# A hybrid Fourier and Hyena encoder layer on one core: real group's inverse transforms once each in fp32, sums by VectorE, and the filters' norms in the gates' convolution taps

## The chip, the cores and the metric

The kernel runs on one core of a Trainium2 chip. A core has five engines that matter here, each with its own queue that it works off in order: TensorE (PE; its weight loads are listed as PEld), VectorE (DVE), ScalarE (ACT), GpSimd (POOL) and SyncE (SP, which here only issues DMA). They share an on-chip memory, SBUF, of 128 partitions; TensorE writes its results to PSUM, from where VectorE and ScalarE read them. The metric is the device time of one execution in microseconds (us), as the median of several runs.

## The reference

The layer is applied to two sequences (x_prompt and x_sample) of 1024 positions and 1024 channels, with the same weights. The Hyena branch is where the change lies:

```python
    h = h * jnp.exp(-t[:, None, None, None] * jnp.abs(decay.astype(f32))[None])
    h = h / jnp.sum(jnp.abs(h), axis=(0, 1), keepdims=True)
    ...
    hv = short_conv(hv, w_short)
    v, x1, x2 = jnp.split(hv, 3, axis=-1)
    kf = hyena_filters(L, ...)
    z = v.astype(jnp.float32)
    for n, gate in enumerate((x1, x2)):
        z = gate.astype(jnp.float32) * long_conv(z, kf[:, n], hyena_d[n].astype(jnp.float32))
    y_h = (z.astype(dt) * jax.nn.silu(hg)) @ w_hyena_out
```

Each filter is divided by its norm, the sum of its absolute values over all positions and both directions, one number per order n and channel. `short_conv` is a depthwise convolution of width 3 over the sequence, `long_conv` a convolution of full length through a Fourier transform of 2048 points plus a skip term. Since the norm is one number per channel, and the short convolution is linear in its taps, the division can be done anywhere on the way to the product with the gate. Around this branch stand a Fourier branch, sigmoid merge gates, an output projection and norms; they are not touched.

## The kernel before

The work stands in stages: the Fourier branch and the norm of the input, then the filters with some of the gates' projections between them (up to some 700 us), then the convolutions (`branches`, about 705 to 1690 us), the remaining gate projections (`phase_gates`) and the output (`phase_out`).

Matrices that need more than one fp32r matmul gives are split: `split` makes a rounded high part h (a ScalarE cast) and a remainder l (a subtraction on VectorE, some on GpSimd), and `mm3` multiplies as h·H + h·L + l·H, three matmuls. Input projections (`inproj`, output tile pin) are 48 such matmuls of 512 columns for a tile of 128 channels.

`branches` runs through 32 steps: two batches, eight channel tiles c, two orders n. A step's long convolution has a front and a back. `conv_front` folds the sequence into even and odd parts, transposes them on TensorE (tph) and makes from them, in `butterfly`, the inputs of four frequency groups: group 0 is real, with one tile of fp32 numbers; groups 2, 1 and 3 are complex and split into bh and bl. `conv_back` (line 796) takes the groups in the order 0, 2, 1, 3. For each, `forward` multiplies with a cosine and sine table into PSUM (pX). Group 0 does that in true fp32 with four matmuls of 128 columns against the table cfw0 (line 596), the others with twelve fp32r matmuls of 256 columns. VectorE multiplies pX with the filter's spectrum (t, line 806) and adds (Y, line 810). Y is split into yh and yl (line 813), and twelve fp32r matmuls of 256 columns transform it back into PSUM (pT, line 833). For group 0 the table holds the cosine part of pair 0 used for both halves by broadcast, and that of pair 4 with both signs, so that PSUM ends with sum and difference next to each other. ScalarE copies the result to T0s (line 839); VectorE later forms U and V from T0s and group 2's result, and S and D from T1s and group 3's, then four sums q and the unfolded output y (yc).

A gate x1 or x2 is a projection, after which `conv` (line 754) applies the three taps of `wsh`: one ScalarE activation with the middle tap, two VectorE instructions for the outer ones. `gate` (line 862) multiplies the convolution's output with the gate and with `invn`, the reciprocal of the filter's norm, in one scalar_tensor_tensor on VectorE. `invn` is a tile of 16 columns, one per order and channel tile, filled by `filter_taps` (line 656), whose last column is written before the convolutions begin.

PSUM tiles named pT and tph come from one pool (tag "T") of two buffers, which are taken in turn: the two transposes of a front, then groups 0, 2, 1, 3 of a back. So group 1's transform writes to the bank that group 0's result was in. Tiles pX have two buffers of their own, pin two.

The order on each engine is not the order of this text. A scheduler places the instructions by an own estimate of their durations when the kernel is built, so a change of a few instructions can move others around it. SP issues the loads of filter spectra (k) and of weights, POOL computes the remainders of the projections' weights and stores and loads some of them.

Of the kernel before, what the change touches and what calls it, by code (L numbers as in the profile page):

```python
# [16 lines left out]
P = 128  # L17
# [29 lines left out]
def _tables():  # L47
    t = {}
    s = np.arange(P) + 0.5
    fwd, inv = [], []  # L50
    th = np.zeros((P, 8, 6))
    for pi, (f1, hf) in enumerate(PAIRS):
# [9 lines left out]
        if f1 == 0:  # L62
            inv += [ci, -si]
        elif f1 == 4:
            inv += [ci, -ci, -si, si]
        else:
            inv += [-si, ci, si]
# [10 lines left out]
    t["c_fwd"] = _hl(np.concatenate(fwd[4:], axis=1))  # L78
    t["c_inv"] = _hl(np.concatenate(inv, axis=1))
# [63 lines left out]
for _pi, (_f1, _hf) in enumerate(PAIRS):  # L143
    IOFF[_pi] = _o
    _o += 256 if _f1 == 0 else (512 if _f1 == 4 else 384)
# [16 lines left out]
class K:  # L162
# [633 lines left out]
    def conv_back(self, n, ct, B, ws):  # L796
# [3 lines left out]
        for g, pairs in GROUPS:  # L800
# [8 lines left out]
            Y = ws.tile([P, 2, 2, P], F32, tag="y", name="y", bufs=1)  # L809
            self.add("dve", Y, t[:, 0], t[:, 1, :, ::-1])  # L810
            yh = ws.tile([P, 2, 2, P], F32R, tag="yh", name="yh", bufs=2)
# [4 lines left out]
            for r in range(2):  # L816
                for i, pr in enumerate(pairs):
                    w = (yh[:, i, r], yl[:, i, r])
                    o = IOFF[pr]
                    if g == 0:  # L820
                        out = T4[:, r::2]
                        if i == 0:
                            R = [ci[:, hl, o + r * P:o + r * P + P].unsqueeze(1).to_broadcast([P, 2, P]) for hl in range(2)]
                        else:
                            R = [ci[:, hl, o + r * 256:o + r * 256 + 256].rearrange("p (a b) -> p a b", a=2)
                                 for hl in range(2)]
                    elif r == 0:
                        out = T4[:, 0::3]
                        R = [ci[:, hl, o + P:o + 3 * P].rearrange("p (a b) -> p a b", a=2) for hl in range(2)]
                    else:  # L830
                        out = T4[:, 1:3]
                        R = [ci[:, hl, o:o + 2 * P].rearrange("p (a b) -> p a b", a=2) for hl in range(2)]
# [4 lines left out]
            if g in (0, 1):  # L837
                T[g] = tt(f"T{g}s")
# [23 lines left out]
    def gate(self, n, ct, y, g):  # L862

        c = n * 8 + ct
        self.stt("dve", g, y, self.invn[:, c:c + 1], g, MUL, MUL)
        return g

    def phase_main(self, nct=8, nb=NB, nf=16):
        tc, nc, a = self.tc, self.nc, self.a
        with ExitStack() as es:  # L870
# [24 lines left out]
            for i in range(nf):  # L895
# [7 lines left out]
                if i == 2:  # L903
                    self.cinv = mi.tile([P, 2, INVW], F32R, name="cinv")
                if i in (2, 4, 6):
# [5 lines left out]
    def branches(self, nb, nct, ws):  # L911
# [3 lines left out]
        tc, nc = self.tc, self.nc  # L915
        steps = []
# [552 lines left out]
```

## Time and profile before

| what | value |
|---|---|
| median of 3 runs | 2442.94 us (2442.49 to 2445.35) |
| the profiled execution's own time | 2444.67 us |
| its span, first to last instruction | 2442.9 us |
| mean granted TensorE clock | 0.996 |
| TensorE busy | 2396.8 us (98%), 13196 matmul records |
| VectorE busy | 1896.5 us (78%) |
| ScalarE busy | 1096.7 us (45%) |
| GpSimd busy | 487.0 us (20%) |
| convolutions' transforms back (pT) | 1024 records with yh, 512 with yl |

The span is 2442.9 us, and the execution as a whole took 1.8 us more. Busy time counts the time in which an engine has at least one instruction under way; matmuls overlap, so the number of a group's records times their mean length is more than the group's time, and what a matmul costs is the distance from its start to the next one's. An fp32 matmul leaves two records, an fp32r matmul one. In rows of the timeline stand start, length, engine, source line, operation, tiles out<-in, shape and count; in rows by stage the stage's bounds and length, and for each engine busy time and count, then the granted clock, the share of the DMA engines and GB/s; in rows of waits, who waited for whom, the sum in us, how often, and the longest.

### The profile page before, as it was taken

The numbers are of one execution on the slowest core, as the hardware profiler recorded it, in microseconds if no ns is written. First come the engines' busy times: TensorE is split into PE (matmuls) and PEld (weight loads), VectorE is DVE, ScalarE is ACT, GpSimd is POOL, SyncE is SP. The second block draws the span as 40 slices with busy tenths as digits, with TensorE's granted clock in tenths as the row PEclk, the third lists the DMA queues.
The fourth block names the chain that finished last, engine by engine and source line by source line (L and its number), as shares of the span: only waits on it lengthen the run. The fifth ranks groups of instructions, "written<-read, shape, count | busy, mean of one in ns | idle before, by whom it ended". The sixth has DMA issues, their size and how long they took to land.

```text
span 2442.9 us, 36854 instructions
## 1 busy us (share of the span) xinstructions
PE 2396.8 (98%) x13196; PEld 2084.8 (85%) x13196; DVE 1896.5 (78%) x3405; ACT 1096.7 (45%) x2063; POOL 487.0 (20%) x518
## 2 busy tenths in 40 slices
PE   6999999999999999999999999999999999999998
PEld 5988888888888888888888888888788888888886
DVE  7687888888748999999989999766555455665677
ACT  5546577767633433334223323333344444544343
POOL 1341322222143433331000000112200012122111
PEclk9999999999999999999999999999999999999999
DMA  7535655555555555545444444335454567776543
GB/s 265 187 133 198 218 180 169 169 176 166 172 194 178 172 177 173 163 165 195 147 129 133 141 141 139 121 121 184 141 177 167 190 211 254 253 255 217 170 162 130
DMA packets 225823, 429.36 MB, mean 176 GB/s; under 512 B 23574, under 2 KB 87287, under 8 KB 225256
## 3 DMA queue, kind: packets, MB, share of 16 engines
q1 hardware_dynamic: 198444, 333.34, 42.5%
q0 software_dynamic: 27008, 93.65, 11.1%
q8 instruction: 104, 1.70, 0.3%
q14 instruction: 79, 0.65, 0.1%
q10 hardware_dynamic: 188, 0.02, 0.0%
HBM read 290.60 MB, written 136.31 MB: 175 GB/s over the span
## 4 chain that ended last, share of the span: by engine, by line
PE 92%; DMA 2%; DVE 2%; ACT 1%; issue 1%; POOL 1%; SPq 0%; DVEq 0%; ACTq 0%; POOLq 0%
PE pin L194 41%; PE pT L194 7%; PE pg L194 7%; PE pyf L194 7%; PE pyh L194 7%; PE pX L194 7%; PE po L194 6%; PE pXf L194 3%; PE pfv L194 2%; PE pft L194 1%; PE tph L792 1%; PE tpx L194 1%; DMA x<-in_x 1%; DMA wr<-in_w_fo 0%; DMA d_x<-xg 0%
## 5 line engine op out<-in xcount | busy, mean ns | idle before, releaser
L194 PE MATMUL pin<-xh,wl 128*128 128x512 f32 x1472 | 577.7, 392 | 3.3 <-POOL wl L181 3.3
L194 PE MATMUL pin<-xh,wh 128*128 128x512 f32 x1472 | 577.2, 392 | 0.9 <-DMA wh<-d_w 0.9
L194 PE MATMUL pin<-xl,wh 128*128 128x512 f32 x1472 | 576.2, 392 | 0.4 <-DVE xl L181 0.4
L181 POOL TENSOR_TENSOR wl<-wr,wh 128x512 fp32r<-128x512 f32 x136 | 240.8, 1772 | 1141.9 <-ACT wh L171 1108.1
L171 ACT CAST wh<-wr 128x512 fp32r<-128x512 f32 x264 | 163.5, 620 | 365.0 <-PE pin L194 141.3
L194 PEld LDWEIGHTS pin<-xh,wl 128*128 128x128 f32 x1472 | 277.5, 189 | 55.8 <-POOL wl L181 4.8
L194 PEld LDWEIGHTS pin<-xh,wh 128*128 128x128 f32 x1472 | 277.4, 188 | 52.5 <-DMA wh<-d_w 1.3
L194 PEld LDWEIGHTS pin<-xl,wh 128*128 128x128 f32 x1472 | 277.5, 189 | 52.2 <-DVE xl L181 1.0
L194 PE MATMUL pT<-cinv,yh 128*128 128x256 f32 x1024 | 193.1, 283 | 0.0
L194 PEld LDWEIGHTS pT<-cinv,yh 128*128 128x128 f32 x1024 | 164.0, 190 | 9.0
L181 DVE TENSOR_TENSOR t<-pX,k 128x1024 f32<-128x1024 f32 x128 | 155.7, 1216 | 11.0 <-PE pX L194 9.3
L181 DVE TENSOR_TENSOR wl<-wr,wh 128x512 fp32r<-128x512 f32 x128 | 87.8, 687 | 94.1 <-ACT wh L171 93.8
L194 PE MATMUL pX<-bh,cfwd 128*128 128x256 f32 x768 | 159.6, 286 | 0.0
L194 PE MATMUL pyf<-sf,wh 128*128 128x512 f32 x512 | 157.7, 389 | 0.0
L194 PE MATMUL pyh<-sh,wh 128*128 128x512 f32 x512 | 157.3, 389 | 0.0
L171 ACT CAST bh<-b 128x512 fp32r<-128x512 f32 x144 | 89.0, 620 | 126.0 <-DVE b L181 84.2
L194 PE MATMUL pT<-cinv,yl 128*128 128x256 f32 x512 | 144.9, 283 | 0.0
L171 ACT CAST yh<-y 128x512 fp32r<-128x512 f32 x128 | 79.2, 618 | 112.3 <-DVE y L181 89.5
L194 PEld LDWEIGHTS pX<-bh,cfwd 128*128 128x128 f32 x768 | 126.4, 190 | 2.5
L194 PEld LDWEIGHTS pyh<-sh,wh 128*128 128x128 f32 x512 | 96.1, 188 | 19.9
L194 PEld LDWEIGHTS pyf<-sf,wh 128*128 128x128 f32 x512 | 96.1, 188 | 19.9
L194 PE MATMUL pX<-bl,cfwd 128*128 128x256 f32 x384 | 109.6, 285 | 0.0
(354 smaller groups left out, 5262.9 us busy)
## 6 DMA issues: line engine op xcount, KB each, us to landing
k<-d_k SPq DMA_DIRECT2D x128, 512.0 KB, 4.0
wr<-in_w_in SPq DMA_DIRECT2D x136, 256.0 KB, 3.1
d_g<-gt SPq DMA_DIRECT2D x124, 256.0 KB, 2.8
d_k<-kt SPq DMA_DIRECT2D x128, 128.0 KB, 2.1
d_k<-kt SPq DMA_DIRECT2D x64, 256.0 KB, 2.3
wr<-in_w_fo POOLq DMA_DIRECT2D x64, 256.0 KB, 4.1
g<-d_g SPq DMA_DIRECT2D x64, 256.0 KB, 4.4
wr<-in_w_ho POOLq DMA_DIRECT2D x64, 256.0 KB, 4.0
```

The source lines that it names most:

```text
L171: self.rounded = nc.scalar.copy(h, src)
L181: return e.tensor_tensor(out, a, b, op=op)
L194: return self.nc.tensor.matmul(out, lhsT, rhs, start=start, stop=stop, skip_group_check=shared)
L792: nc.tensor.transpose(tp[:, q * P:(q + 1) * P], eo[:, e, q], self.ident)
```

## The change

Group 0's inverse tables leave `c_inv` and stand in a table of their own, `c_in0`, in plain fp32, with each of the four pieces once. In `conv_back`, group 0 no longer splits Y. Four fp32 matmuls of 128 columns put the two cosine products pair 0's two products (cosine and sine) side by side into the lower half of a PSUM tile (pT0) and pair 4's into its upper half; ScalarE copies the upper half of 256 columns to T0s, and VectorE adds it to the lower half and subtracts it from it, which gives the two halves of T0s, in the order that they had before. Y of group 0 (y0) lies in a buffer of the yl ring instead of y's only buffer. The tables for `c_inv` shrink from 3072 to 2304 columns in each part, loaded in three DMAs as before; `c_in0` is one more DMA on SP's queue, of 128 x 512 fp32 numbers.

The norms are multiplied once, ahead of the convolutions, into the taps of the sections of x1 and x2 (16 blocks of three columns of `wsh`), and `gate` becomes a plain product on VectorE.

```diff
--- before.py
+++ after.py
@@ -47,7 +47,7 @@
 def _tables():
     t = {}
     s = np.arange(P) + 0.5
-    fwd, inv = [], []
+    fwd, in0, inv = [], [], []
     th = np.zeros((P, 8, 6))
     for pi, (f1, hf) in enumerate(PAIRS):
         f = f1 + 8 * (np.arange(P) + P * hf)
@@ -59,10 +59,8 @@
             wt[0] = 1 / 2048.0
         fwd += [c, sn]
         ci, si = (c * wt).T, (sn * wt).T
-        if f1 == 0:
-            inv += [ci, -si]
-        elif f1 == 4:
-            inv += [ci, -ci, -si, si]
+        if f1 in (0, 4):
+            in0 += [ci, -si]
         else:
             inv += [-si, ci, si]
         ang = w * 127.5
@@ -76,6 +74,7 @@
             th[:, pi] = np.stack([ct, -st, 0 * ct, 0 * ct, st, 0 * ct], axis=1)
     t["c_fw0"] = np.concatenate(fwd[:4], axis=1).astype(np.float32)
     t["c_fwd"] = _hl(np.concatenate(fwd[4:], axis=1))
+    t["c_in0"] = np.concatenate(in0, axis=1).astype(np.float32)
     t["c_inv"] = _hl(np.concatenate(inv, axis=1))
     t["c_th"] = th.astype(np.float32)
 
@@ -142,7 +141,7 @@
 _o = 0
 for _pi, (_f1, _hf) in enumerate(PAIRS):
     IOFF[_pi] = _o
-    _o += 256 if _f1 == 0 else (512 if _f1 == 4 else 384)
+    _o += 0 if _f1 in (0, 4) else 384
 INVW = _o
 GROUPS = [(0, (0, 1)), (2, (4, 5)), (1, (2, 3)), (3, (6, 7))]
 KOFF = {0: 0, 1: 8, 2: 16, 3: 24}
@@ -806,8 +805,21 @@
             self.mul("dve", t.rearrange("p k h r c -> p k (h r c)"),
                      X.rearrange("p h r c -> p (h r c)").unsqueeze(1).to_broadcast([P, 2, 512]),
                      kt.rearrange("p (k a) b -> p k (a b)", k=2))
-            Y = ws.tile([P, 2, 2, P], F32, tag="y", name="y", bufs=1)
+            Y = ws.tile([P, 2, 2, P], F32, tag="y" if g else "yl", name="y" if g else "y0", bufs=1 if g else 2)
             self.add("dve", Y, t[:, 0], t[:, 1, :, ::-1])
+            if g == 0:
+
+                Tp = self.psum("T", 2, "pT0")
+                for i in range(2):
+                    for r in range(2):
+                        s = slice((2 * i + r) * P, (2 * i + r + 1) * P)
+                        self.mm(Tp[:, s], Y[:, i, r], self.cin0[:, s], True, True)
+                T[0] = ws.tile([P, 512], F32, tag="tt", name="T0s", bufs=4)
+                lo, hi = T[0][:, 0:256], T[0][:, 256:512]
+                nc.scalar.copy(hi, Tp[:, 256:512])
+                self.add("dve", lo, Tp[:, 0:256], hi)
+                self.sub("dve", hi, Tp[:, 0:256], hi)
+                continue
             yh = ws.tile([P, 2, 2, P], F32R, tag="yh", name="yh", bufs=2)
             yl = ws.tile([P, 2, 2, P], F32R, tag="yl", name="yl", bufs=2)
             self.split(yh, yl, Y, "dve", "act")
@@ -817,14 +829,7 @@
                 for i, pr in enumerate(pairs):
                     w = (yh[:, i, r], yl[:, i, r])
                     o = IOFF[pr]
-                    if g == 0:
-                        out = T4[:, r::2]
-                        if i == 0:
-                            R = [ci[:, hl, o + r * P:o + r * P + P].unsqueeze(1).to_broadcast([P, 2, P]) for hl in range(2)]
-                        else:
-                            R = [ci[:, hl, o + r * 256:o + r * 256 + 256].rearrange("p (a b) -> p a b", a=2)
-                                 for hl in range(2)]
-                    elif r == 0:
+                    if r == 0:
                         out = T4[:, 0::3]
                         R = [ci[:, hl, o + P:o + 3 * P].rearrange("p (a b) -> p a b", a=2) for hl in range(2)]
                     else:
@@ -834,8 +839,8 @@
 
             def tt(name):
                 return ws.tile([P, 512], F32, tag="tt", name=name, bufs=4)
-            if g in (0, 1):
-                T[g] = tt(f"T{g}s")
+            if g == 1:
+                T[g] = tt("T1s")
                 nc.scalar.copy(T[g], Tp)
             elif g == 3:
                 S_, D_ = tt("S"), T[1]
@@ -861,8 +866,7 @@
 
     def gate(self, n, ct, y, g):
 
-        c = n * 8 + ct
-        self.stt("dve", g, y, self.invn[:, c:c + 1], g, MUL, MUL)
+        self.mul("dve", g, y, g)
         return g
 
     def phase_main(self, nct=8, nb=NB, nf=16):
@@ -902,6 +906,8 @@
                     self.spill_gate(0, sec, c, ws)
                 if i == 2:
                     self.cinv = mi.tile([P, 2, INVW], F32R, name="cinv")
+                    self.cin0 = mi.tile([P, 4 * P], F32, name="cin0")
+                    nc.sync.dma_start(self.cin0, a["c_in0"])
                 if i in (2, 4, 6):
 
                     s = slice((2, 4, 6).index(i) * INVW // 3, ((2, 4, 6).index(i) + 1) * INVW // 3)
@@ -913,6 +919,8 @@
 
 
         tc, nc = self.tc, self.nc
+        gt = self.wsh.rearrange("p (m j) -> p m j", j=3)[:, 8:24]
+        self.mul("dve", gt, gt, self.invn.unsqueeze(2).to_broadcast([P, 16, 3]))
         steps = []
         for b in range(nb):
             steps.append((b, 0, 0))
```

The scheduler's order is another one from the first convolution on. Up to there TensorE's rows are the same, and after the convolutions too. The first place is TensorE at the ninth convolution of the first batch, at group 0's transform back. Before, the end of it and what follows (pX_11229 is group 3's forward transform, pT_11175 group 2's transform back; the twelve matmuls of pT_11137 had begun six rows ahead):

```order
L194 MATMUL pT_11137<-cinv_4030,yh_11133 128x2x128 x2
L194 MATMUL pT_11137<-cinv_4030,yl_11134 128x2x128
L194 MATMUL pX_11229<-bh_10701,cfwd_3076 128x256 x2
L194 MATMUL pT_11175<-cinv_4030,yh_11171 128x2x128 x2
L194 MATMUL pX_11229<-bl_10702,cfwd_3076 128x256
```

And now the same place (pX_11104 is group 1's forward transform, pX_11142 group 3's):

```order
L193 MATMUL pX_11104<-bh_10630,cfwd_3076 128x256 x2
L193 MATMUL pX_11104<-bl_10631,cfwd_3076 128x256
L193 MATMUL pT0_11056<-cin0_4031,y0_11054 128x128 x4
L193 MATMUL pX_11104<-bh_10630,cfwd_3076 128x256
L193 MATMUL pX_11142<-bh_10634,cfwd_3076 128x256
```

The four matmuls of group 0 stand before the end of group 1's forward transform; before, they stood within group 3's.

The second place is VectorE in the same convolution. Before, Y of group 0 (y_11131) and its remainder yl_11134, with other work between them:

```order
L181 TENSOR_TENSOR y_11131<-t_11129 128x512
L181 TENSOR_TENSOR b02_11026<-xt_11012 128x256
L181 TENSOR_TENSOR S_10921<-T1s_10883,pT_10908 128x512
L181 TENSOR_TENSOR t_11167<-pX_11152,k_11165 128x1024
L181 TENSOR_TENSOR yl_11134<-y_11131,yh_11133 128x512
```

Now the addition and the subtraction that make T0s_11061, and what stands between them (x1_10441 is the gate of the convolution before):

```order
L180 TENSOR_TENSOR yl_11085<-y_11082,yh_11084 128x512
L180 TENSOR_TENSOR T0s_11061<-pT0_11056,T0s_11061 128x256
L180 TENSOR_TENSOR bl_10961<-b02_10949,bh_10960 128x512
L180 TENSOR_TENSOR x1_10441<-yc_10855,x1_10441 128x1024
L180 TENSOR_TENSOR b02_10949<-bs_10948 128x2x128 x2
L180 TENSOR_TENSOR y_11121<-t_11119 128x512
L180 TENSOR_TENSOR T0s_11061<-pT0_11056,T0s_11061 128x256
```

Group 0's remainder is gone from the queue; the two new instructions come later in the convolution, five others apart.

The third place is TensorE where the bank of group 0's result is used again, by group 1's transform back (pT_11127):

```order
L193 MATMUL pin_11463<-xh0_1_2969,wl_11465 128x512
L193 MATMUL pX_11311<-b02_10949,cfw0_3075 128x128 x4
L193 MATMUL pin_11463<-xh0_2_2974,wh_11464 128x512
L193 MATMUL pT_11127<-cinv_4030,yh_11123 128x2x128 x2
L193 MATMUL pin_11463<-xl0_2_2975,wh_11464 128x512
```

Between the four matmuls of pT0_11056 and pT_11127 stand 33 matmuls of pin, 13 of pX and 12 of pT (group 2's) with 256 columns, and the four fp32 ones of the next convolution's pX_11311.

## The prediction

> **What bounds the kernel now.** I read the page's first part and its chain of waits, then the busy times by stage, then the waits of the stage that the change touches.
>
> ```profile
> PE 2396.8 (98%) x13196; PEld 2084.8 (85%) x13196; DVE 1896.5 (78%) x3405; ACT 1096.7 (45%) x2063; POOL 487.0 (20%) x518
> PE 92%; DMA 2%; DVE 2%; ACT 1%; issue 1%; POOL 1%; SPq 0%; DVEq 0%; ACTq 0%; POOLq 0%
> ```
>
> TensorE is busy 98% of the span and carries 92% of the chain. But the change lies in the stage of the long convolutions alone (the transforms pT stand between 705 and 1690 us), so its worth is read there. The columns are busy time and instruction count of each engine, then granted clock, DMA share and GB/s:
>
> ```profile
> 705.00:800.00 95.00, 95.00 (x551) 83.72 (x550) 76.05 (x110) 34.10 (x57) 35.55 (x37) 1.00 0.53 167
> 800.00:950.00 150.00, 150.00 (x910) 133.84 (x908) 148.44 (x231) 58.09 (x106) 54.95 (x55) 1.00 0.55 174
> 950.00:1110.00 160.00, 160.00 (x978) 143.04 (x977) 152.47 (x240) 60.01 (x108) 55.19 (x53) 1.00 0.50 162
> 1110.00:1200.00 90.00, 88.70 (x510) 77.11 (x509) 83.41 (x125) 33.00 (x52) 5.58 (x4) 1.00 0.53 171
> 1200.00:1550.00 350.00, 350.00 (x2123) 312.70 (x2123) 323.08 (x523) 108.93 (x193) 4.35 (x3) 1.00 0.43 139
> 1550.00:1690.00 140.00, 140.00 (x784) 122.50 (x783) 93.56 (x146) 41.40 (x75) 25.50 (x18) 1.00 0.40 126
> ```
>
> Two things are to be seen. TensorE (second number) has no gap but 1.3 us in 1110 to 1200. And VectorE (fourth) is close behind: in 800 to 950 it has 150 - 148.44 = 1.56 us left, in 950 to 1110 it has 7.5, in 1200 to 1550 it has 26.9. The list of TensorE's waits from 705 to 1690 us is these two rows, and nothing else:
>
> ```profile
> PE pin L194 <- DMA wh<-d_w: 0.9, 1, 0.9
> PE pin L194 <- DVE xl L181: 0.4, 1, 0.4
> ```
>
> So no matmul of a convolution waits for VectorE today. TensorE's matmul time is the bound, and VectorE the next one, with almost no room in one stretch.
>
> **The change part by part. TensorE.** Each convolution's real group (g = 0) now has twelve fp32r matmuls of 256 columns in its inverse transform; it gets four fp32 matmuls of 128 columns. What such matmuls cost is their pace, not the length of a record, since they overlap. Weight loads of one transform of twelve in a row (2+1+2+1+2+1+2+1), start, length, count at the end:
>
> ```profile
> 904.82 0.31 PEld L194 LDWEIGHTS pT<-cinv,yh 128*128 128x128 f32 x2
> 905.06 0.19 PEld L194 LDWEIGHTS pT<-cinv,yl 128*128 128x128 f32 x1
> ...
> 906.26 0.31 PEld L194 LDWEIGHTS pX<-bh,cfwd 128*128 128x128 f32 x2
> ```
>
> From 904.82 to 906.26 is 1.44 us for the twelve, 0.12 each. All four groups have this shape. The four new matmuls have the shape and type of the real group's forward transform, which the trace shows:
>
> ```profile
> 914.94 0.98 PEld L194 LDWEIGHTS pX<-b,cfw 128*128 128x128 f32 x8
> 915.84 0.19 PEld L194 LDWEIGHTS pin<-xh,wh 128*128 128x128 f32 x1
> 915.95 0.19 PEld L194 LDWEIGHTS pin<-xl,wh 128*128 128x128 f32 x1
> 916.18 0.19 PEld L194 LDWEIGHTS pin<-xh,wl 128*128 128x128 f32 x1
> ```
>
> Four fp32 matmuls leave eight records, and these take 915.84 - 914.94 = 0.90 us. The saving is 1.44 - 0.90 = 0.54 us a convolution. There are 32 of them (two batches, two orders, eight channel tiles): **17.3 us** of TensorE time, if nothing else sets the pace.
>
> **VectorE.** It loses the subtraction that makes yl (512 elements) and gains an addition and a subtraction of 256 elements each, with one input in PSUM. Its pace on such sizes, from start to start:
>
> ```profile
> 905.42 1.21 DVE L181 TENSOR_TENSOR t<-pX,k 128x1024 f32<-128x1024 f32 x1
> 906.55 0.67 DVE L181 TENSOR_TENSOR bl<-b,bh 128x512 fp32r<-128x512 f32 x1
> 907.15 0.41 DVE L177 SCALAR_TENSOR_TENSOR q<-ez,T0s 128x256 f32<-128x256 f32 x1
> 907.48 0.41 DVE L177 SCALAR_TENSOR_TENSOR q<-ez,U 128x256 f32<-128x256 f32 x1
> 907.82 0.68 DVE L181 TENSOR_TENSOR yl<-y,yh 128x512 fp32r<-128x512 f32 x1
> 908.42 1.28 DVE L181 TENSOR_TENSOR yc<-q 128x512 f32<-128x512 f32 x2
> L177 DVE SCALAR_TENSOR_TENSOR x<-yc,invn,x x20: 1271/1277/2319, 1110.3 to 1688.3; 128x1024 f32<-128x1024 f32 x20
> L177 DVE SCALAR_TENSOR_TENSOR x<-yc,invn,x 128x1024 f32<-128x1024 f32 x32 | 48.1, 1502 | 0.1
> ```
>
> 256 elements take 0.34 us, 512 take 0.60. So +0.68 - 0.60 = +0.08 a convolution. The gate goes from scalar_tensor_tensor (median 1.277) to a plain product of 1024 elements (1.21 as in the row of t): -0.07. VectorE's work stays as it is, within 0.01 us a convolution; where VectorE would become the bound, the change gives it nothing. Its bounds by rows: the gates' mean is 1.502, so -0.21 if all that lies over 1.21 goes away, and +0.08 if the gate gains nothing. I take zero, since the median gate is short and the long ones are long by what runs beside them.
>
> Some of these instructions run far over their median:
>
> ```profile
> L181 DVE TENSOR_TENSOR yl<-y,yh x128: 672/681/1672, 732.8 to 1676.3; 128x512 fp32r<-128x512 f32 x128
> L181 DVE TENSOR_TENSOR S<-T1s,pT x32: 670/686/689, 752.4 to 1681.9; 128x512 f32<-128x512 f32 x32
> ```
>
> The subtraction with both inputs in SBUF reaches 1.672 us, the one with an input in PSUM never passes 0.689. [...]
>
> **How VectorE's lack of room cuts the gain.** The instructions on T0s by stretch; ScalarE's (second count) is the copy, one a convolution:
>
> ```profile
> 705.00:800.00 95.00, 4.38 (x8) 1.74 (x3) 1.00 0.53 167
> 800.00:950.00 150.00, 12.26 (x22) 2.92 (x5) 1.00 0.55 174
> 950.00:1110.00 160.00, 11.73 (x22) 3.51 (x6) 1.00 0.50 162
> 1110.00:1200.00 90.00, 7.57 (x12) 1.17 (x2) 1.00 0.53 171
> 1200.00:1550.00 350.00, 25.86 (x48) 7.03 (x12) 1.00 0.43 139
> 1550.00:1690.00 140.00, 8.84 (x17) 2.34 (x4) 1.00 0.40 126
> ```
>
> In 800 to 950 TensorE would be 5 x 0.54 = 2.7 us quicker, but VectorE has 1.56 us to give: 1.1 us is lost. In 950 to 1110 it needs 6 x 0.54 = 3.2 of 7.5, and after 1110 18 x 0.54 = 9.7 against far more. These fit.
>
> **ScalarE** loses the rounding of yh and copies 256 columns of PSUM in place of 512. It is at 58.09 of 150 us at its fullest stretch; nothing is counted. **The chain within a convolution:** Y reaches TensorE without ScalarE's and VectorE's two steps, but the result leaves PSUM later. Rows of ScalarE's copies of about these sizes:
>
> ```profile
> L839 ACT COPY T0s<-pT 128x512 f32<-128x512 f32 x32 | 18.7, 585 | 39.5 <-PE pT L194 31.8 <-DVE ez L181 5.3 <-DVE q L177 2.4
> L431 ACT COPY sev<-pse 128x258 f32<-128x258 f32 x16 | 6.0, 375 | 7.0 <-DVE x L181 2.0 <-DVE sst L437 1.7 <-PE pse L194 1.7
> ```
>
> Before, one copy of 0.585 us freed the bank; now 0.375, then two VectorE instructions. In the order of the ninth convolution bl, the gate, two b02 and y stand between these two: by the paces 0.60 + 1.13 + 0.68 + 0.60 = 3.0 us, so the bank is held 0.375 + 0.34 + 3.0 + 0.41 = 4.1 us. The next user of the bank is the transform of g = 1. TensorE's own work up to it is 33 matmuls of pin (0.23 each, the last two rows of the loads above), 25 of pT and pX of 256 columns and four fp32: 7.6 + 3.0 + 0.9 = 11.5 us. That cover hides the longer hold with 7.4 us to spare; if it were gone, TensorE would wait up to 3.5 us a convolution.
>
> **Once only.** The product of the taps with the norms is one instruction of 48 elements, behind the last reciprocal, before 705 us: under the 0.34 us of 256 elements, on an engine that isn't the bound there. The c_in0 load (256 KB) stands on SP's queue between loads of filters and weights; the c_inv loads on POOL's shrink by a quarter. TensorE's order before 705 us and after the stage is unchanged. Nothing counted.
>
> **Sum.** 17.3 - 1.1 = 16.2 us, against the profiled span of 2442.9 us: 2426.7. That execution's own time was 2444.67, 1.8 over its span; the median of the runs is 2442.94, so I take the saving as a difference from it: **2426.7 us**.
>
> **The rivals.** *VectorE sets the pace to 1110 us.* It has 1.56 us in the fullest stretch and no instruction is cut there; if the rest of its idle time is wait that can't be squeezed, the 14 convolutions up to 1110 gain nothing and the other 18 gain 9.7: 2433.2. For it speaks the row of 800 to 950, against it the 19 us that VectorE idles in 705 to 800 and the 7.5 after 950.
>
> *VectorE sets the pace up to 1550.* Only the last four convolutions gain, 2.2 us: 2440.7, no change that can be told (0.2%, 4.9 us, is about what a measurement of this kernel can tell from none). Against it: 26.9 us of idle VectorE time in 1200 to 1550.
>
> *The held bank, slower.* VectorE, in order, comes late to the addition, which waits for ScalarE's copy; behind it stand bl, the gate and the next convolution's front, and TensorE's g = 1 transform waits for the bank. It decides once VectorE lags by more than the 7.4 us above, and turns the sign where the wait passes 0.54 us a convolution. At 1 us each: 2442.9 + 32 x 0.46 = 2457.6. For it: 98 to 99% of VectorE in 800 to 950; against: no such wait today. A long wait would cost more than itself, as the next stage shows:
>
> ```profile
> PE pin L194 <- POOL wl L181: 3.0, 2, 1.9
> 1710.00:1730.00 20.00, 17.31 (x75) 14.06 (x76) 11.54 (x9) 7.42 (x9) 9.42 (x5) 1.00 0.62 213
> 1730.00:1750.00 20.00, 20.00 (x83) 16.33 (x82) 11.83 (x13) 6.85 (x10) 2.63 (x5) 0.91 0.40 133
> ```
>
> After 2.7 us without matmuls in 20 the clock was granted at 0.91 over the next 20, 1.8 us lost. [...]
>
> *The fp32 matmuls are dearer than the forward ones.* If the eight records took a 512-column pace, 0.23 each, a convolution would lose 1.84 - 1.44 = 0.40: 2455.7. Against it stands the same shape and type in the row of pX.
>
> **How the numbers follow.** Forecast 0.60, its own range 2424 (17.3 and the 1.3 us of waits gained as well, with VectorE lighter by its bound) to 2430 (half of the early gain lost). VectorE to 1110: 0.19. VectorE to 1550: 0.11. Held bank: 0.08. Dear fp32: 0.02. Faster is the first two, 0.79; same 0.11; slower 0.10. The range 2421 to 2441 holds the first three and leaves out the last two, and a little of their neighbours for costs not seen.
>
> **What would show it.** The g = 0 transforms as 256 records at 0.9 us for eight; about 128 fewer weight loads (256 where there were 384); TensorE without a gap from 705 to some 1674 us and its stage 16 us shorter; VectorE's share there up to 99% in the fullest stretch, with no row "PE pT <- DVE" among the waits. Wrong would be: rows in which pT or pX waits for VectorE for more than 5 us in sum, eight records over 1 us, or a shift before 705 us.

## The result, and the profile after

The changed kernel takes **2427.4 us** (median of 6 runs, 2425.56 to 2429.1) against 2443.3 us before (6 runs beside them): a ratio of **0.9934, 95% interval 0.9921 to 0.9947**, or 16 us less. The profiled execution took 2427.36 us. Its page begins so:

```profile
span 2425.6 us, 36573 instructions
PE 2377.9 (98%) x13068; PEld 2065.0 (85%) x13068; DVE 1908.2 (79%) x3438; ACT 1071.8 (44%) x2031; POOL 478.7 (20%) x518
```

There are 128 matmul records fewer and 18.9 us less busy time on TensorE, and 11.7 us more busy time on VectorE, although its work was to stay as it was (the account of the prediction comes back to this). The weight loads of one new transform in the timeline show its price:

```profile
844.24 0.98 PEld L193 LDWEIGHTS pT<-cin,y 128*128 128x128 f32 x8
845.14 0.19 PEld L193 LDWEIGHTS pX<-bh,cfwd 128*128 128x128 f32 x1
```

845.14 - 844.24 = 0.90 us for the eight records of four fp32 matmuls. Next, the stage of the convolutions and the hand-over after it. First the rows by stage of the kernel before, cut at the first pX, at the end of the last pT and at the first gate matmul pg (bounds and length, then busy time and count of TensorE, its weight loads, VectorE, ScalarE and GpSimd, then the granted clock, DMA share and GB/s):

```profile
705.10:1681.80 976.70, 975.40 (x5807) 866.04 (x5806) 869.25 (x1357) 333.12 (x586) 176.26 (x161) 1.00 0.47 151
1681.80:1741.50 59.70, 56.71 (x241) 46.07 (x241) 39.17 (x39) 21.31 (x28) 20.60 (x15) 0.97 0.62 212
```

The same two stretches of the changed kernel:

```profile
703.80:1668.10 964.30, 959.14 (x5681) 849.26 (x5680) 881.83 (x1389) 309.61 (x556) 168.00 (x162) 1.00 0.48 154
1668.10:1722.40 54.30, 54.30 (x240) 44.64 (x240) 36.34 (x36) 20.03 (x26) 18.77 (x14) 1.00 0.63 224
```

So the 17.3 us between the two spans (2442.9 and 2425.6) lie here:

| stretch | before | after | difference |
|---|---|---|---|
| to the first pX | 705.1 | 703.8 | -1.3 |
| stage of the convolutions | 976.7 | 964.3 | -12.4 |
| hand-over, to the first pg | 59.7 | 54.3 | -5.4 |
| from there to the end | 701.4 | 703.2 | +1.8 |

The stage itself gives 12.4 us and not 16.2. TensorE now idles 964.30 - 959.14 = 5.16 us in it; before it was 976.70 - 975.40 = 1.30. The list of its waits in the stage of the changed kernel:

```profile
PE pin L193 <- DVE xl L180: 2.0, 2, 1.4
PE pT L193 <- ACT yh L170: 1.9, 1, 1.9
PE tph L791 <- DVE T0s L180: 0.9, 1, 0.9
PE pT L193 <- DVE yl L180: 0.2, 1, 0.2
PE pX L193 <- DVE t L180: 0.2, 1, 0.2
```

All of them go back to VectorE (what yh waited for is shown below). A name in this list can stand for more than one instruction. T0s is written by the two new ones of 256 columns, and also by the subtraction of 512 that makes V in T0s's place from T0s and group 2's result, which the kernel before has too. The one that released this tph is the latter:

```profile
834.05 0.67 DVE L180 TENSOR_TENSOR T0s<-T0s,pT 128x512 f32<-128x512 f32 x1
```

In the rows by stage the waits fall into the middle:

```profile
705.00:800.00 95.00, 95.00 (x545) 83.50 (x544) 80.34 (x118) 31.97 (x56) 34.18 (x38) 1.00 0.51 164
800.00:950.00 150.00, 149.08 (x910) 133.13 (x909) 149.64 (x231) 54.42 (x99) 52.89 (x54) 1.00 0.57 180
950.00:1110.00 160.00, 157.90 (x945) 139.85 (x944) 159.18 (x247) 55.58 (x102) 49.88 (x52) 1.00 0.51 162
1110.00:1200.00 90.00, 87.86 (x502) 76.36 (x501) 80.58 (x127) 30.84 (x50) 7.16 (x3) 1.00 0.51 173
```

VectorE is busy 149.64 of 150 us, and then 159.18 of 160: it has 0.36 and 0.82 us left. Before, it had 7.5 us in the second of these stretches.

The hand-over is 5.4 us shorter, which nothing in the prediction foresaw. Before, it had the wait of 3.0 us for GpSimd's wl (quoted in the prediction) and a mean clock of 0.97; after it has no idle time at all and a clock of 1.00. 3.0 us are the wait, 59.7 x 0.03 = 1.8 us the clock, and the rest is two input matmuls that stand ahead of the last pT now (239 records of pin in the hand-over where there were 241), 0.23 us each; these are in the stage's time instead. Right behind the hand-over the changed kernel has two waits, 1.2 us in sum, where there were none; they are part of the 1.8 us by which the last stretch is longer.

### The profile page after: what moved, and what is told of

Its sections match the earlier page's. It is cut to its first block, busy times and chain, and to the rows that moved or that the text cites. A ratio compares the mean times of both kernels' runs of the same rounds, so it can differ in the third digit from the quotient of the medians.

```text
span 2425.6 us, 36573 instructions
## 1 busy us (share of the span) xinstructions
PE 2377.9 (98%) x13068; PEld 2065.0 (85%) x13068; DVE 1908.2 (79%) x3438; ACT 1071.8 (44%) x2031; POOL 478.7 (20%) x518
## 3 DMA queue, kind: packets, MB, share of 16 engines
q0 software_dynamic: 27008, 92.86, 11.1%
## 5 line engine op out<-in xcount | busy, mean ns | idle before, releaser
L180 POOL TENSOR_TENSOR wl<-wr,wh 128x512 fp32r<-128x512 f32 x136 | 233.1, 1714 | 1126.0 <-ACT wh L170 1088.7
L193 PE MATMUL pT<-cinv,yh 128*128 128x256 f32 x768 | 145.0, 284 | 1.9 <-ACT yh L170 1.9
L193 PEld LDWEIGHTS pT<-cinv,yh 128*128 128x128 f32 x768 | 123.1, 190 | 8.3 <-ACT yh L170 2.3
L170 ACT CAST yh<-y 128x512 fp32r<-128x512 f32 x96 | 59.5, 620 | 124.6 <-DVE y L180 113.9
L193 PE MATMUL pT<-cinv,yl 128*128 128x256 f32 x384 | 109.3, 285 | 0.2 <-DVE yl L180 0.2
```

The source lines that it names most:

```text
L170: self.rounded = nc.scalar.copy(h, src)
L180: return e.tensor_tensor(out, a, b, op=op)
L193: return self.nc.tensor.matmul(out, lhsT, rhs, start=start, stop=stop, skip_group_check=shared)
```

## The experiments

Each kernel's stage, cut in the same way, and the time at the median; "idle" is the stage's length minus TensorE's busy time. The last column is the sum by which VectorE's elementwise instructions between 700 and 1110 us exceed the 10th percentile of their own kind (same operation, tiles and shape), called **excess** below. It is worked out from all records of the trace.

| kernel | time, us | ratio to before | stage, us | idle, us | excess, us |
|---|---|---|---|---|---|
| before | 2443.3 | 1 | 976.7 | 1.3 | 24.0 |
| after | 2427.4 | 0.9934 [0.9921, 0.9947] | 964.3 | 5.2 | 35.1 |
| before, again (one run) | 2440.6 | - | 976.7 | 1.6 | 23.6 |
| after, again | 2427.3 | 0.9936 [0.9923, 0.9949] | 964.3 | 4.0 | 33.8 |
| norms alone | 2442.4 | 1.0005 [0.9996, 1.0013] | 978.0 | 1.5 | 27.7 |
| fp32 alone | 2425.7 | 0.9938 [0.9924, 0.9952] | 964.3 | 4.3 | 32.5 |
| fp32 matmuls twice | 2459.5 | 1.0075 [1.0060, 1.0089] | 995.7 | 6.9 | 36.0 |
| no sums | 2425.2 | 0.9938 [0.9925, 0.9951] | 963.8 | 4.2 | 28.9 |
| one VectorE addition more | 2426.9 | 0.9942 [0.9930, 0.9955] | 966.1 | 5.1 | 36.7 |
| bank freed at once | 2427.2 | 0.9939 [0.9926, 0.9951] | 965.1 | 4.7 | 31.4 |
| no remainders by GpSimd | 2417.6 | 0.9901 [0.9885, 0.9917] | 957.3 | 0.0 | 9.0 |
| products by VectorE | 2419.4 | 0.9904 [0.9890, 0.9919] | 958.8 | 0.8 | 19.4 |
| products by VectorE, before | 2442.7 | 1.0003 [0.9994, 1.0012] | 977.7 | 2.0 | 17.7 |

### The two halves of the change apart

The kernel before with the norms alone:

```diff
-        c = n * 8 + ct
-        self.stt("dve", g, y, self.invn[:, c:c + 1], g, MUL, MUL)
+        self.mul("dve", g, y, g)
...
+        gt = self.wsh.rearrange("p (m j) -> p m j", j=3)[:, 8:24]
+        self.mul("dve", gt, gt, self.invn.unsqueeze(2).to_broadcast([P, 16, 3]))
```

> Only the norms go into the taps; group 0's transform stays at twelve fp32r matmuls. Theory (TensorE's matmul time sets the pace): no matmul is saved, VectorE gets 0.07 us lighter a convolution where TensorE never waited for it, so 2443 us, within 2 us of before, and the two POOL waits at the hand-over to the gate projections (3.0 us) may come or go with the new order. Rival (the shorter gate on VectorE carries a good part of the gain): 2436 us or less.

The changed kernel with the norms put back into the gates, so that only the transform of group 0 differs from before:

```diff
-        self.mul("dve", g, y, g)
+        c = n * 8 + ct
+        self.stt("dve", g, y, self.invn[:, c:c + 1], g, MUL, MUL)
...
-        gt = self.wsh.rearrange("p (m j) -> p m j", j=3)[:, 8:24]
-        self.mul("dve", gt, gt, self.invn.unsqueeze(2).to_broadcast([P, 16, 3]))
```

> Only group 0's transform in fp32 with VectorE's sums; the gate stays a scalar_tensor_tensor with the norm. Theory: the 17.3 us of matmul time are saved as in the full change, VectorE is 0.07 us heavier a convolution, which costs up to 1 us in the full stretch from 800 to 1110 us: 2427 to 2430 us. Rival (the gate carries a part): 2434 us or more.

Norms alone: 2442.4 us, ratio 1.0005. fp32 alone: 2425.7 us, ratio 0.9938, a little under what was expected. So the whole gain comes with the transform, and the norms are worth nothing that can be told. That holds although the gates did get shorter on VectorE (32 products of mean 1.333 us in the changed kernel, where there were 32 of 1.502), and although the one new instruction is as small as thought. Rows of VectorE in the changed kernel, the first by group (busy, mean ns, idle before), the second with minimum, median, maximum, first and last start:

```profile
L180 DVE TENSOR_TENSOR x<-yc,x 128x1024 f32<-128x1024 f32 x32 | 42.7, 1333 | 0.2
L180 DVE TENSOR_TENSOR wsh<-wsh,invn x1: 197/197/197, 643.4 to 643.4; 128x48 f32<-128x48 f32 x1
```

The 32 gates are 5.4 us shorter in sum (32 x 0.169). In the kernel with the norms alone they are 8.1 us shorter (mean 1.249) and bought no time, where VectorE has room. Between fp32 alone (mean 1.348) and the whole change they differ by 0.5 us in sum, so what a shorter gate is worth where VectorE has no room isn't shown.

### Does TensorE set the pace?

Each of the four fp32 matmuls is issued twice, the second overwriting the first with the same values:

```diff
                         self.mm(Tp[:, s], Y[:, i, r], self.cin0[:, s], True, True)
+                        self.mm(Tp[:, s], Y[:, i, r], self.cin0[:, s], True, True)
```

> The changed kernel with the four fp32 matmuls issued twice, each time from fresh: 0.90 us more TensorE time a convolution, 28.7 us in all, and nothing more on VectorE. Theory: TensorE sets the pace, and where it waited for VectorE (about 6 us in the stage) the added work fills the waits: 2427 + 28.7 - 4 to 0 = 2452 to 2456 us, with the waits gone. Rival (VectorE sets the pace of the stage since the change): a good part of the 28.7 is hidden, 2440 us or less.

It took 2459.5 us, above both. The stage is 995.7 - 964.3 = 31.4 us longer. The doubled matmuls are 32 x 0.90 = 28.8 us of that, so every microsecond of them is paid: TensorE sets the pace, as the theory had it. But the waits did not go away, as they should have if TensorE now left VectorE 0.9 us a convolution more; idle time rose from 5.2 to 6.9 us. The waits of this kernel:

```profile
PE pT L193 <- DVE T0s L180: 5.5, 3, 2.9
PE pin L193 <- DVE xl L180: 1.0, 2, 0.8
PE pT L193 <- DVE y L180: 0.4, 1, 0.4
```

The first row names T0s, but it is not the bank that group 0 holds longer. All three matmuls were released by the subtraction that makes V; the longest one, with its row of VectorE and its own:

```profile
954.56 0.68 DVE L180 TENSOR_TENSOR T0s<-T0s,pT 128x512 f32<-128x512 f32 x1
955.38 0.55 PE L193 MATMUL pT<-cinv,yh 128*128 128x256 f32 x1 [2.94 <-DVE T0s L180]
```

The two new instructions on T0s of this convolution were over long before, the second at 943.44 us. VectorE was late at V, behind two instructions b that took 4.85 us together and a yl of 2.23 us. This speaks for waits that are single events, not the difference of two sums of work, and that fall where instructions come to stand beside each other.

### Is it VectorE's load, or the held bank?

Three edits of the same place. First, ScalarE copies all of the transform and VectorE's sum and difference are left out (the real group's sum and difference are not computed), 0.68 us less VectorE work a convolution, and the bank free after one copy:

```diff
-                nc.scalar.copy(hi, Tp[:, 256:512])
-                self.add("dve", lo, Tp[:, 0:256], hi)
-                self.sub("dve", hi, Tp[:, 0:256], hi)
+                nc.scalar.copy(T[0], Tp)
```

> The changed kernel without VectorE's addition and subtraction for group 0; ScalarE copies all 512 columns of the transform to T0s as they are, so the real group's sum and difference are left out of what is computed. VectorE is 0.68 us lighter a convolution, TensorE as in the changed kernel. Theory: the new waits of TensorE for VectorE between 800 and 1140 us (about 4.5 us more than before the change) go away: 2422 to 2425 us. Rival (those gaps come from the order or from DMA, not from VectorE's load): 2427 us, unchanged. Rival (VectorE sets the pace): 0.68 us on 14 or more convolutions, 2417 us or less.

Second, one VectorE addition of 256 elements more in each convolution, whose result nobody reads:

```diff
                 self.sub("dve", hi, Tp[:, 0:256], hi)
+                ex = ws.tile([P, 256], F32, tag="ex5", name="ex5", bufs=1)
+                self.add("dve", ex, lo, hi)
```

> The changed kernel with one VectorE addition more a convolution (256 elements, both inputs in SBUF, 0.34 us; its result is not used). Theory: in the full stretch from 800 to 1110 us there are 11 convolutions, 3.7 us, and this is all on TensorE's path; in the rest VectorE has room: 2 to 5 us over the changed kernel, 2429 to 2432 us. Rival (TensorE's waits hang on single collisions, not on VectorE's sum): within 1.5 us of the changed kernel. Rival (VectorE sets the pace everywhere): 32 x 0.34 = 11 us more.

Third, the same sums, but from a copy in SBUF, so that the bank is free after ScalarE's copy:

```diff
-                nc.scalar.copy(hi, Tp[:, 256:512])
-                self.add("dve", lo, Tp[:, 0:256], hi)
-                self.sub("dve", hi, Tp[:, 0:256], hi)
+                ab = ws.tile([P, 512], F32, tag="ab6", name="ab6", bufs=1)
+                nc.scalar.copy(ab, Tp)
+                self.add("dve", lo, ab[:, 0:256], ab[:, 256:512])
+                self.sub("dve", hi, ab[:, 0:256], ab[:, 256:512])
```

> The changed kernel with all 512 columns of group 0's transform copied out of PSUM by ScalarE (0.59 us), and VectorE's addition and subtraction made from SBUF: the bank is free after the copy, as before the change, and the two instructions have both inputs in SBUF. Theory: the waits of TensorE for T0s (0.9 us of 5) go away, but the two instructions can now be stretched by GpSimd too: within 2 us of the changed kernel. Rival (the longer hold of the bank is what cost the gain): 3 to 5 us faster, about 2423 us.

Without the sums it took 2425.2 us. In the trace VectorE has more room (145.08 of 150 us busy where it was 149.64), but the waits stay, at other places:

```profile
PE pT L193 <- DVE yl L180: 1.3, 2, 0.7
PE pin L193 <- DVE xl L180: 1.1, 1, 1.1
PE tph L791 <- DVE eo L180: 0.9, 1, 0.9
PE pX L193 <- DVE t L180: 0.7, 2, 0.4
...
800.00:950.00 150.00, 148.32 (x903) 132.32 (x902) 145.08 (x225) 55.53 (x99) 59.80 (x54) 1.00 0.56 178
```

The time, 2425.2 us, is the upper end of what the theory expected, and its ratio can't be told from the changed kernel's; but the waits were to go away and did not. So VectorE's sum of work is not what makes them: 21.8 us of it (32 x 0.68) can go, and 4.2 us of idle time on TensorE remain. One addition more gave 2426.9 us, the same time within the interval, with a stage 1.8 us longer in the one profiled execution: too little to settle anything by itself, and less than a kernel paced by VectorE's load should show. Its longest waits are again for V:

```profile
PE pT L193 <- DVE T0s L180: 2.3, 2, 1.5
```

With the bank freed at once it took 2427.2 us, as the theory had it. No wait for T0s is in its list, and others have come in their place:

```profile
PE pin L193 <- DVE xl L180: 2.7, 1, 2.7
PE pT L193 <- DVE yl L180: 1.2, 1, 1.2
PE pin L193 <- POOL wl L180: 0.8, 2, 0.5
```

Group 0's held bank therefore isn't the cost either: freeing it gains nothing, and in no run did a matmul wait directly for one of the two new instructions (by over 0.15 us, below which the lists show no wait).

### Is it GpSimd running beside VectorE?

The timeline around the longest wait in the changed kernel pointed to a third theory. VectorE there (start, length, then the instruction):

```profile
1085.02 0.67 DVE L180 TENSOR_TENSOR U<-T0s,pT 128x512 f32<-128x512 f32 x1
1085.61 4.67 DVE L180 TENSOR_TENSOR eo<-x 128x512 f32<-128x512 f32 x2
1090.21 0.75 DVE L180 TENSOR_TENSOR b<-xt,bs 128x256 f32<-128x256 f32 x2
```

GpSimd in the same microseconds:

```profile
1085.39 1.28 POOL L180 TENSOR_TENSOR wl<-wr,wh 128x512 fp32r<-128x512 f32 x1 [2.77 <-ACT wh L170]
1087.19 2.54 POOL L180 TENSOR_TENSOR x<-x,sg 128x512 f32<-128x512 f32 x2
```

And ScalarE behind it:

```profile
1091.66 0.62 ACT L170 CAST bh<-b 128x512 fp32r<-128x512 f32 x1 [5.38 <-DVE b L180]
1092.27 0.62 ACT L170 CAST yh<-y 128x512 fp32r<-128x512 f32 x1
```

Two instructions eo took 4.67 us together, where the two instructions yc, of the same size, took 1.28 us in the prediction's row of the kernel before. For 3.6 of these 4.67 us GpSimd ran its subtraction and its two products beside them. ScalarE, in order, waited 5.38 us for b, and yh, which TensorE wanted, stood behind it: that is the wait of 1.9 us. To test it, GpSimd's load beside the convolutions is taken away in two ways. First, the remainder of each weight is written by ScalarE as a second cast instead of by GpSimd as a subtraction (the remainder is left out of the computation, which changes no count of matmuls):

```diff
-                self.split(*parts, r, "pool", "act")
+                self.rounded = nc.scalar.copy(parts[0], r)
+                self.left = nc.scalar.copy(parts[1], r)
```

> The changed kernel without GpSimd's subtractions for the input projections' weights: ScalarE casts the weights a second time into the remainder's place, so the remainder is left out of what is computed. VectorE's instruction list is the same, but nothing beside it on GpSimd reads SBUF but the 16 products with sg. Theory (the new waits come from VectorE instructions that are stretched by GpSimd's, 36 us in sum over 700 to 1110 us, not from their number): the stretching falls to under 12 us, TensorE's waits before 1110 us go away, 3 to 4 us faster than the changed kernel. Rival (order or VectorE's plain load): as the changed kernel, within 1.5 us.

Second, the 16 products of the merge gates, 512 elements each, go from GpSimd to VectorE, on top of the whole change; nothing of what is computed changes:

```diff
-                    self.mul("pool", X[i][:, s], X[i][:, s], sg[q])
+                    self.mul("dve", X[i][:, s], X[i][:, s], sg[q])
```

> The changed kernel with the 16 products of a gate with sg on VectorE (512 elements, 0.60 us each, 9.6 us in sum) in place of GpSimd (1.27 us or more each). Theory (GpSimd's readers cost VectorE about as much as they save it): within 2 us of the changed kernel, either way. Rival (VectorE's plain load alone decides): the 14 of them in the full stretch, 8.4 us, show in the time, 5 to 8 us slower than the changed kernel.

Both kernels of the main comparison ran again beside them, on the same chip:

> The kernel before, unchanged, for a second profile beside those of the other kernels. In the first one TensorE took 60.0 us from the last transform of a convolution to the first matmul of the gate projections, with 3.0 us of waits for POOL in it; the three builds with other orders that I have looked at need 54.4 to 55.2. Theory (the order on POOL and ScalarE at the hand-over makes that wait, so it belongs to this build): 59 to 60 us again, about 2441 us. Rival (it differs from execution to execution): some 55 us.

> The changed kernel, unchanged, on the same chip as the others of this call, so that they are compared with it and not with a number from another chip. Theory: 15 to 17 us under before; TensorE's waits in the convolutions again about 5 us, at the same places.

The repeats agree with the first runs: 2427.3 us after, 2440.6 us in the one run before, and stages of 964.3 and 976.7 us, to the tenth the same as in the first traces. The hand-over differs, and it says which part of the unforeseen 5.4 us can be counted on. In the repeat of the kernel before it is 57.0 us, at full clock:

```profile
1680.60:1737.60 57.00, 55.03 (x241) 44.89 (x240) 37.52 (x37) 21.21 (x28) 20.59 (x15) 1.00 0.64 222
```

That lies between the two expectations. The waits for wl were 2.0 us there, and no clock was lost; so 2.7 of the 5.4 us come back, 2.7 were that execution's. The prediction put the lost clock of the first one down to the waits; what cost it isn't shown.

Without GpSimd's remainders the kernel takes 2417.6 us, 9.7 less than the changed one beside it. Expected were 3 to 4 if GpSimd was the cause. Its stage by row, and two VectorE groups from 705 to 1110 us (busy, mean ns, idle before):

```profile
800.00:950.00 150.00, 150.00 (x912) 133.81 (x911) 145.07 (x237) 63.45 (x117) 26.94 (x38) 1.00 0.55 183
950.00:1110.00 160.00, 160.00 (x957) 142.24 (x956) 149.19 (x246) 65.61 (x122) 26.85 (x34) 1.00 0.50 163
...
L180 DVE TENSOR_TENSOR eo<-x 128x512 f32<-128x512 f32 x14 | 9.0, 681 | 0.0
L180 DVE TENSOR_TENSOR b<-xt,bs 128x256 f32<-128x256 f32 x28 | 10.6, 415 | 0.0
```

TensorE never waits in the stage, VectorE has 4.9 and 10.8 us left, and these two groups have their undisturbed lengths. This edit also moves work to ScalarE, and it gained more than the theory can claim. The stage is 964.3 - 957.3 = 7.0 us shorter, where TensorE's idle time was 4.0 to 5.2 us; the spans differ by another 2.9 us, most of it (1.7) behind the hand-over. No run says where the surplus comes from.

With the products on VectorE the kernel takes 2419.4 us, 8.0 less than the changed kernel beside it. **It is faster than both kernels: 0.9904 [0.9890, 0.9919] of the time before.** Both expectations were wrong: the theory had it within 2 us of the changed kernel, and the rival, by which VectorE's load decides, 5 to 8 us slower. Its rows by stage, the only wait of TensorE in the stage, and the two groups that answer:

```profile
800.00:950.00 150.00, 150.00 (x907) 133.76 (x906) 147.41 (x233) 54.80 (x98) 51.28 (x51) 1.00 0.56 180
950.00:1110.00 160.00, 160.00 (x967) 142.44 (x966) 156.63 (x256) 55.81 (x102) 46.65 (x43) 1.00 0.52 162
...
PE pin L193 <- DMA wh<-d_w: 0.7, 1, 0.7
...
L180 DVE TENSOR_TENSOR eo<-x 128x512 f32<-128x512 f32 x14 | 11.5, 862 | 0.0
L180 DVE TENSOR_TENSOR x<-x,sg 128x512 f32<-128x512 f32 x14 | 9.2, 680 | 0.0
```

VectorE has these 14 instructions on top up to 1110 us, 9.2 us of work, and yet is busy less in 950 to 1110 (156.63 us where it was 159.18). On GpSimd the same products had taken 20.4 us. In the changed kernel:

```profile
L180 POOL TENSOR_TENSOR x<-x,sg 128x512 f32<-128x512 f32 x14 | 20.4, 1477 | 7.4 <-ACT sg L962 7.3
```

### Is that edit worth as much without the change?

The same line in the kernel before:

> The kernel before (twelve fp32r matmuls for group 0, gate with the norm) with the 16 products of a gate with sg on VectorE instead of GpSimd. Theory: before the change TensorE waits for nothing in the convolutions but 1 to 2 us at the change of batch, so a VectorE that is less stretched has nothing to give: within 2 us of before. Rival (moving these products is a gain of its own, 8 us, that has nothing to do with the change): 2434 us.

2442.7 us, ratio 1.0003 [0.9994, 1.0012]: worth nothing. There, too, the excess fell, from 24.0 to 17.7 us, but no matmul had waited for it. The move pays only after the change has used up VectorE's room.

## Why the prediction was right, and where it was not

The time came out 0.7 us from the forecast, and its bound, TensorE's matmuls, is the right one. But that it came so close is luck, since misses cancel in it: of the two spans' 17.3 us the stage gives 3.8 less than the 16.2 forecast, the hand-over 5.4 that were not forecast, and the rest of the kernel 1.3 more and 1.8 less.

**The matmul term (17.3 us) was right.** Eight records take 0.90 us, and doubling them costs all of their time. The cleanest check is the kernel with the products on VectorE, where the stage has almost no wait: it is 976.7 - 958.8 = 17.9 us shorter than before, of which 0.5 are idle time, so 17.4 are matmul time. (Two input matmuls more stand in it than before, so the term is known to some 0.5 us.)

**The norms at nothing: right,** as the two halves apart show. The gate lost 0.17 us (1.502 to 1.333) of the 0.29 that its bound allowed; with 0.08 for the sums that is -0.09 a convolution, inside the bounds of -0.21 and +0.08, and no effect on the time can be told.

**The step that failed is the sentence on the stretches after 950 us, "These fit", and with it "1.1 us is lost" as the whole loss.** By TensorE's idle time the loss was 5.16 - 1.30 = 3.9 us: 0.9 in 800 to 950, near the 1.1 of the prediction, but 2.1 in 950 to 1110, which was said to fit, and 0.8 more in 1110 to 1200. (17.3 - 3.9 is 13.4, and the stage gave 12.4; the two input matmuls are 0.5 of that, and 0.5 is not accounted for.) The sum took VectorE's room in the kernel before and its work at its pace, and from these worked out what would be left. But VectorE's durations are no constants. From 705 to 1110 us, before, two of its groups were

```profile
L181 DVE TENSOR_TENSOR eo<-x 128x512 f32<-128x512 f32 x14 | 9.0, 679 | 0.0
L181 DVE TENSOR_TENSOR b<-xt,bs 128x256 f32<-128x256 f32 x26 | 9.8, 414 | 0.0
```

and after the change, the same counts of the same instructions,

```profile
L180 DVE TENSOR_TENSOR eo<-x 128x512 f32<-128x512 f32 x14 | 14.1, 1046 | 0.0
L180 DVE TENSOR_TENSOR b<-xt,bs 128x256 f32<-128x256 f32 x26 | 18.0, 728 | 0.0
```

13.3 us more in two groups that the change does not touch. In the new order these stand beside GpSimd's instructions, where others stood before: from 705 to 1110 us eo overlaps GpSimd's arithmetic for 5.7 us and b for 11.1, where it was nothing and 2.4. Over all instructions from 700 to 1110 us the excess rose from 24.0 to 35.1 us, about what VectorE's busy time grew by. In the changed kernel 33.6 of the 35.1 us lie in the 152 instructions that overlap an arithmetic instruction of GpSimd, and all 34 that run more than a quarter over their undisturbed length are among these. Those with an input in PSUM are not stretched even there: the 53 that overlap GpSimd's work are 0.2 us over in sum, the sixteen t among them 0.1. The prediction showed this difference in two rows of the kernel before (yl up to 1.672 us, S never over 0.689) and took nothing from it for the instructions that the change does not touch. The two new ones, with an input in PSUM, do stay short (T0s has a median of 0.41 us and a maximum of 0.42). The question to ask was which of the other instructions would stand beside GpSimd's in the new order, and which side would lose by it. They do not meet for longer: VectorE's instructions without an input in PSUM overlap GpSimd's arithmetic for 62 us before and 63 us after, from 700 to 1110 us. But in this time VectorE's excess went from 22 to 33 us, while GpSimd's arithmetic got shorter, from a mean of 1.76 us to 1.62.

That GpSimd's work beside VectorE makes the waits is borne out by the two kernels that lessen it: TensorE's idle time goes from 5.2 to 0.0 and 0.8 us, one of them with more work on VectorE. In every kernel with the new transform and an excess of 28 us or more there were 4 to 7 us of idle time; in both with less than 20 there was next to none. Without the remainders the two sides overlap for 16 us; with the products on VectorE it is still 55 us, but there GpSimd pays more of it (its remainders take 1.88 us in the mean, where they took 1.66). What isn't shown is why an order brings the two together and which side then loses: the order is made anew for each kernel, and no run kept the new order while changing only that. So an order that happens to be kinder isn't ruled out as a part of what these two kernels gained.

**The held bank.** Its price, reckoned at 1 us a convolution, counts no lost clock: waits of 0.9 and 0.4 us from 1110 to 1200 us before stood at a granted clock of 1.00. It was never paid: no wait ends with one of the two new instructions, in any run, and freeing the bank at once gains nothing. The rows that name T0s (0.9 us in the changed kernel, 5.5 with the matmuls doubled, 2.9 with one addition more) are V's, which reads group 2's result, as it did before the change. The 7.4 us of cover for group 0's bank held, although they were worked out with VectorE's undisturbed paces and a pair that is stretched to 4.67 us takes 3.4 of them.

```profile
L180 DVE TENSOR_TENSOR T0s<-pT,T0s x64: 404/412/424, 732.2 to 1655.4; 128x256 f32<-128x256 f32 x64
L819 ACT COPY T0s<-pT x32: 362/373/374, 731.3 to 1654.6; 128x256 f32<-128x256 f32 x32
```

The sizes of both, 0.41 and 0.37 us, were as forecast.

**What cancelled it.** "TensorE's order before 705 us and after the stage is unchanged. Nothing counted" was wrong as well, to the other side: the hand-over is 5.4 us shorter in the pair of profiled executions, 2.7 against the repeat. The wait for wl at GpSimd was there to be read in the prediction's own quoted row and was used only to price a rival; that it could go away when the order changes was not asked. The kernel with the norms alone has a shorter hand-over too (54.9 us), and 1.3 us more in its stage: five input matmuls more stand in its stage (236 records of pin in its hand-over). Such a shift can come with an edit that saves no matmul.

**What would have shown it.** The 256 records at 0.90 us and the fewer weight loads came as said, and VectorE went up to 99%, indeed 99.8%. "TensorE without a gap", no row "PE pT <- DVE" and "its stage 16 us shorter" did not: TensorE waits six times in the stage, one of them in a row of that kind (0.2 us), and the stage is 12.4 us shorter. The bound that would have refuted it, over 5 us of pT or pX waiting for VectorE, was not reached: with yh, which waited for VectorE's b, they are 2.3 us. The first pX is 1.3 us earlier than before, and a shift before 705 us was named as a sign of being wrong; but the kernel before, run again, has it at 703.9 us too, so this comes and goes with the execution.

## What to carry to other kernels

When an engine stands at 98% of a stretch or more, as VectorE did here (148.44 of 150 us before the change, 149.64 after), its room can't be read from the undisturbed durations of its instructions: first subtract each group's shortest length from its mean, and see what runs beside the long ones, since the next order of the instructions will mix them anew. Work given to GpSimd is not free for VectorE: here the kernel was 8.0 us faster with 16 products on VectorE than with them on GpSimd, but only once VectorE's room was gone. A row of waits goes by a tile's name, and more than one instruction can write that tile: look up which one released the matmul before a theory is built on the name. And a total that comes out right is no proof of its terms; compare stage by stage.

## What was not expected of the hardware

Two VectorE instructions of 512 elements took 4.67 us in place of some 1.28, beside GpSimd instructions of 1.27 us each, so that VectorE lost 4.67 - 1.28 = 3.4 us in 3.6 us of overlap, nearly all of it. And moving 14 products of 0.68 us to VectorE left it less busy in 950 to 1110 us than before (156.63 for 159.18).
